# A two-layer encoder on one core: channel vectors behind the second weight block, bias tables negated once and fetched a slice early, a shared slot in each triangle

## The chip, the cores and the metric

The kernel runs on one core of one Trainium2 chip. The metric is the device time of one execution in microseconds, as the median of several runs. The kernel is one launch without loops on the device: the Python code is unrolled into 24029 instructions.

## The reference

Two post-norm layers over a sequence of 512 rows of 1024 channels, float32. In each layer one wide projection of the input feeds three mixers, whose results are projected, gated, summed, projected again, added to the input and normalised. A SwiGLU feed-forward part follows. Cut to its frame, with the part that the change touches:

```python
for l in range(DEPTH):
    h = einsum('bsd,de->bse', x, w_in[l])
    rq, rk, rv, rg, cq, ck, cv, dq, dk, dv, gates = split(h, splits)
    o_a = _retention(...)                    # 4 heads
    o_b = _chunk_attention(cq, ck, cv, ca_rel_bias[l])   # 8 heads
    o_c = _diff_attention(...)               # 4 heads, two softmaxes each
    g = sigmoid(gates + b_merge[l])
    merged = g[0] * (o_a @ w_a) + g[1] * (o_b @ w_b) + g[2] * (o_c @ w_c)
    x = _layer_norm(ALPHA * x + merged @ w_out[l], ln1_g[l], ln1_b[l])
    u_gate, u_up = split(x @ w_ffn_in[l])
    x = _layer_norm(ALPHA * x + (silu(u_gate) * u_up) @ w_ffn_out[l], ln2_g[l], ln2_b[l])

# in _chunk_attention, per head: a bias that depends on query minus key alone
idx = clip(qpos + pad - kpos, -REL_CLIP, REL_CLIP) + REL_CLIP
s = q @ k.T * d ** -0.5 + rel_bias[:, idx]
p = softmax(where(valid, s, -1e30))
```

## The kernel before

Every product runs in three matmuls (`mm3`, L108): each float32 operand is carried as a pair of float32r tiles, a high part that ScalarE casts (`part_hi`, L91) and a low part that VectorE subtracts (`part_lo`, L97). A weight block of up to 128x2048 (`Wt`, L113) is loaded by a DMA on the SyncE queue (SP) into a staging slot, one of 3, and split into `wh` (ScalarE, L138) and `wl` (VectorE, L139), 3 slots each.

The work is a list of items, written out by hand (L993 to L1009). Each item has one to three weight blocks and a function. `run_items` (L472) loads weight blocks so that three are ahead, calls the function, and lets it call `between()` in its middle and at its end, which emits the next group of side work (a head's softmax, a transposition and so on). So the program's order on each engine comes from this list. A scheduler at compile time then puts the instructions of each engine's queue in order by this program order and by when it reckons their inputs ready, so that one with ready inputs can go ahead of earlier ones; each queue runs in that order on the chip.

Activation tiles of 128x512 come from one pool of 61 slots (`g`, L75). A tile that finds no free slot waits, and so does what is queued behind its first instruction.

**The start** (`u_first`, L581). In layer 0, `run_items` first loads the first weight block in four pieces with the eight tiles of the transposed input between them (`load_x`, `split_x`), then the second and third block. Then `whole` (L591) loads two rotary tables (`ret_tables`, L564), emits `vectors()` (L523), and then projects by the first block: for each of the 8 input tiles k, six matmuls. The projections by the second and third block follow, 48 matmuls each. In layer 1 `halves` (L603) does it in halves of the columns, since the input comes out of the layer norm in halves.

`vectors()` loads seven rows of channel vectors with small DMAs (L531), clears their tile on GpSimd first (L526), turns them with one TensorE transpose (`pcol`, L535), copies the result out (L537), and derives a halved gate bias `hb` (L541), which the third block's gates need, and a scalar from four more DMAs (`lv`, L546).

**The chunk attention.** Its eight heads run as three slices each, `s_c1`, `s_c2`, `s_c3`, spread over nine items by `c(i)` (L977): in the middle of item i, `s_c3` of head i-2 and `s_c1` of head i; at its end `s_c2` of head i-1. The items are by turns a branch projection `u_branch(0, .)` and a query and key projection `u_cqk(.)`, then `u_vhl(dv)` and `u_dqk(0)`.

- `s_c1` (L785) loads the head's bias table `tb` as 128 overlapping rows of 512 out of one row of 768 (L789), negates it on ScalarE (L790), sets one corner (L791), and takes scores (`psc`, TensorE), the biased minimum (L350, VectorE), exp (L352, ScalarE) and the scaling by the sums (L799).
- `s_c2` (L803) transposes the triangle of scores (`ptr`, L365) and splits it into three pairs `cP`, six slots: blocks of 512, 512 and 256 columns.
- `s_c3` (L809) multiplies by the values (`pco`, L824), which waits for these splits.

**Gates.** The tanh tiles of some gates (`EARLY`, L45) are stored to memory and loaded again. `u_branch` (L955) calls `gate_of` (L941) for both of its halves first, so both loads (L945) come ahead of the first projection; L966 uses the tile after each.

Retention and differential attention have the same six-slot triangles (`s_r1`, L689; `s_d2`, L879).

Of the kernel before, what the change touches and what calls it, by code (L numbers as in the profile page):

```python
# [12 lines left out]
F32 = mybir.dt.float32  # L13
F32R = mybir.dt.float32r
# [3 lines left out]
P = 128  # L18
# [38 lines left out]
def trunk(ctx, tc, x_in, xT_in, w_in, ret_norm_g, da_norm_g, lq1, lk1, lq2, lk2, w_a, w_b, w_c, b_merge, w_out,  # L57
# [14 lines left out]
    nc.gpsimd.memset(mhalf, -0.5)  # L72
    saved = [dram.tile([S, D], F32, name=f"saved{i}") for i in range(2 * DEPTH - 1)]

    def g(dt=F32, name="g"):  # L75
        return gp.tile([P, 512], dt, tag="g", name=name)

# [6 lines left out]
    class Pair:  # L84


        def __init__(self, name="pr"):
            self.hi = g(F32R, name + "h")
            self.lo = g(F32R, name + "l")

    def part_hi(hi, src, scale=None):  # L91
        if scale is None:
# [420 lines left out]
    def layer(l):  # L513
# [6 lines left out]

        v = {}

        def vectors():  # L523

            rows = small.tile([64, P], F32, tag="rows", name="rows", bufs=1)
            nc.gpsimd.memset(rows, 0.0)  # L526
            r0 = 0
            for name, ap in (("bm", b_merge), ("rg", ret_norm_g), ("dg", da_norm_g), ("g1", ln1_g), ("b1", ln1_b),
                             ("g2", ln2_g), ("b2", ln2_b)):
                n = ap.shape[1] // P  # L530
                nc.sync.dma_start(rows[r0:r0 + n], ap[l:l + 1].rearrange("o (r c) -> (o r) c", c=P))  # L531
                v[name] = slice(r0, r0 + n)
                r0 += n
            psc = bank("pcol")
            nc.tensor.transpose(psc[:, :64], rows, ident[:64, :64])  # L535
            colv = small.tile([P, 64], F32, tag="colv", name="colv", bufs=2)
            nc.scalar.copy(colv, psc[:, :64])  # L537
            for name in list(v):
                v[name] = colv[:, v[name]]
            hb = small.tile([P, 24], F32, tag="hb", name="hb", bufs=2)  # L540
            nc.vector.tensor_scalar_mul(hb, v["bm"], 0.5)  # L541
            v["hb"] = hb

            lv = small.tile([P, 4, DA_DH], F32, tag="lv", name="lv", bufs=1)
            for j, vec in enumerate((lq1, lk1, lq2, lk2)):
                nc.sync.dma_start(lv[:, j], vec[l:l + 1].to_broadcast([P, DA_DH]))  # L546
            lp = small.tile([P, 2, DA_DH], F32, tag="lp", name="lp", bufs=1)
            for j in range(2):
                nc.vector.tensor_mul(lp[:, j], lv[:, 2 * j], lv[:, 2 * j + 1])
            ls = small.tile([P, 2], F32, tag="ls", name="ls", bufs=1)  # L550
            nc.vector.tensor_reduce(ls, lp, axis=mybir.AxisListType.X, op=ALU.add)
            le = small.tile([P, 2], F32, tag="le", name="le", bufs=1)
            nc.scalar.activation(le, ls, AF.Exp)
            nlam = small.tile([P, 1], F32, tag="nlam", name="nlam", bufs=2)
            nc.vector.tensor_sub(nlam, le[:, 1:2], le[:, 0:1])
            nc.vector.tensor_scalar_add(nlam, nlam, -lambda_init)
            v["nlam"] = nlam
# [23 lines left out]
        def u_first():  # L581

            def done(i, j, ps):
                if (i, j) == (0, 0):
                    xq.update({k: Quarters(xT[k], xT[k + 4]) for k in range(4)})
                if i < 2:
                    rqk_done((rq, rk)[i], j, ps)
                else:
                    gate_done(0, j, ps)

            def whole(*wts):  # L591
                ret_tables()
                vectors()
                banks = [bank("pt") for _ in range(2)]
                for k in range(KT):
                    for j in range(2):
                        a, c = xT[k], slice(P * j, P * j + P)
                        mm3(banks[j], wts[0].hi[:, k, c], wts[0].lo[:, k, c], a.hi, a.lo, k == 0, k == KT - 1)
                for i, w in enumerate(wts):
                    for j in range(2):  # L600
                        done(i, j, proj_T(xT, w, P * j) if i else banks[j])

            def halves(*wts):  # L603
                ret_tables()
                vectors()
                banks = [[bank("pt") for _ in range(2)] for _ in wts[:2]]
                proj_T_half0(xT, [(w, P * j, p[j]) for w, p in zip(wts, banks) for j in range(2)], {})
                banks.append([bank("pt") for _ in range(2)])
                proj_T_half0(xT, [(wts[2], P * j, banks[2][j]) for j in range(2)],
                             {2 * b: functools.partial(hooks[l], b) for b in range(4)})  # L610
                for i, (w, p) in enumerate(zip(wts, banks)):
                    for j in range(2):
                        done(i, j, proj_T(xT, w, P * j, ps=p[j], half=1))

            fn = whole if l == 0 else halves
            return [([wcols(c, 256)], KT) for c in (RQ, RK, GATE)], fn
# [68 lines left out]
        def s_r1(h):  # L685
            def fn():
                dh = g(name="dh")
                nc.sync.dma_start(dh, decay[h])
                rp[h] = [Pair("rp") for _ in range(3)]  # L689
                q, k = rq.pop(h), rk.pop(h)  # L690
                for b in range(3):
                    tmp = g(name="rtmp")
                    for mt in range(NT):
                        if PACK[mt][0] != b:
                            continue
                        o, w = PACK[mt][1], S - P * mt
                        ps = bank("psr")
                        msl = slice(P * mt, P * mt + P)
                        mm3(ps[:, :w], k.hi[:, msl], k.lo[:, msl], q.hi[:, P * mt:], q.lo[:, P * mt:], True, True)
                        nc.vector.tensor_mul(tmp[:, o:o + w], ps[:, :w], dh[:, :w])  # L700
                    w = PACKW[b]
                    split(rp[h][b], tmp[:, :w], cols=slice(0, w))
            return fn
# [67 lines left out]
            per = 256 // wd  # L771
            return dst[mt, h // per], (h % per) * 2 * wd

        cv, cqk, cE, cP = {}, {}, {}, {}
        ob = [None] * 4

        def u_cqk(p):
# [4 lines left out]
                cqk[p].set_k(proj_T(xT, wt, P))  # L782
            return [([wcols(CQ + P * p, P), wcols(CK + P * p, P)], KT)], fn

        def s_c1(h):  # L785
            def fn():
                tb = g(name="tb")
                src = rel[l, h:h + 1, 0:1]
                nc.sync.dma_start(tb, bass.AP(src.tensor, src.offset, [[1, P], [1, 512]]))  # L789
                nc.scalar.mul(tb, tb, -1.0)  # L790
                nc.vector.memset(tb[0:64, 0:64], -NEG)  # L791
                E = [g(name="cE") for _ in range(3)]
                sums = softmax_num(cqk[h // 2], h % 2, tb, E)
                r = small.tile([P, NT], F32, tag="rec", name="rec")
                nc.vector.reciprocal(r, sums)
                for nt in range(NT):
                    pk, c = PACK[NT - 1 - nt]
                    e = E[pk][:, c:c + P * (nt + 1)]
                    nc.vector.tensor_scalar_mul(e, e, r[:, nt:nt + 1])  # L799
                cE[h] = E  # L800
            return fn

        def s_c2(h):  # L803
            def fn():
                cP[h] = [Pair("cP") for _ in range(3)]
                transpose_triangle(cE.pop(h), cP[h])
            return fn

# [67 lines left out]

        def s_d2(h):
            def fn():
                dP[h] = [Pair("dP") for _ in range(3)]  # L879
                transpose_triangle(dE.pop(h), dP[h])  # L880
            return fn

# [72 lines left out]
        def u_branch(br, i):  # L955
            w = (w_a, w_b, w_c)[br][l]
            nk = w.shape[0] // P

            def fn(wt):
                act = (oa, ob, oc)[br]  # L960
                ts = [gate_of(br, 2 * i + j) for j in range(2)]
                for j in range(2):
                    d = 2 * i + j
                    ps = proj_T(act, wt, P * j, nk=nk)
                    t = ts[j]
                    nc.vector.scalar_tensor_tensor(t, t, 1.0, ps, op0=ALU.add, op1=ALU.mult)  # L966
                    if br == 0:
                        acc[d] = t
                    else:
                        nc.vector.tensor_add(acc[d], acc[d], t)  # L970
                    if br == 2:
                        mg[d] = Pair("mg")
                        split(mg[d], acc.pop(d), scale=0.5)
                    between()
            return [([w[:, 256 * i:256 * i + 256]], nk)], fn
# [306 lines left out]
```

## Time and profile before

| | |
|---|---|
| time, three runs | median 1947.54 us (1946.57 to 1952.31) |
| profiled execution | 1950.65 us, of which the span of instructions is 1948.8 us |
| mean granted TensorE clock | 0.998 |
| moved by DMA | 240.95 MB, 124 GB/s over the span |
| busy, of the span | TensorE 98%, weight loads 83%, VectorE 67%, ScalarE 45%, GpSimd 2% |

TensorE's row is the one to start from: it is nearly never idle, so a change can only pay where it removes one of its pauses or its work. For a pause, the profile names the instruction after it and what ended it. A matmul's busy time overlaps the next one's, so the pace of matmuls is read from the distance of their starts. A wait of another engine costs nothing by itself; it counts where TensorE's next instruction hangs on it.

### The profile page before, as it was taken

What the parts mean: (1) busy time and instruction counts of PE and PEld (TensorE: products, weight loads), DVE (VectorE), ACT (ScalarE), POOL (GpSimd) and SP (SyncE); (2) the same over time, 40 slices, a digit from 0 to 9 for tenths busy, and PEclk for the clock granted to TensorE, in tenths of its full rate; (3) what the DMA queues carried; (4) which work ended last, traced back from release to release, by engine and by line L of the source; (5) the groups of instructions that cost most, each with busy time, mean ns of one, the idle gap of its engine ahead of it and who ended that gap; (6) DMA issues with size and microseconds to landing.
All of it is one profiled execution on the core that took longest, in us unless ns stands there. A gap on an engine that the chain in (4) does not pass through costs nothing. (4 is left out here: it accounts for less than half of the span.)

```text
span 1948.8 us, 24029 instructions
## 1 busy us (share of the span) xinstructions
PE 1910.1 (98%) x9250; PEld 1608.0 (83%) x9250; DVE 1305.7 (67%) x2182; ACT 885.9 (45%) x1567; POOL 44.3 (2%) x73
## 2 busy tenths in 40 slices
PE   6999999999999999999999999999999999999998
PEld 5888887788888888888898888777888888888886
DVE  5776756667766756656578777566677557675666
ACT  4444445566743433333255454455676343333330
POOL 0000000000000000000000000000000000000000
PEclk9999999999999999999999999999999999999999
DMA  7353533222235434534434534331331634444341
GB/s 233 126 177 114 168 108 103 82 87 71 71 119 168 145 94 154 153 108 141 140 119 165 181 130 123 116 107 55 98 97 44 206 97 152 129 151 131 98 132 51
DMA packets 241782, 240.95 MB, mean 124 GB/s; under 512 B 8078, under 2 KB 180228, under 8 KB 241668
## 3 DMA queue, kind: packets, MB, share of 16 engines
q1 hardware_dynamic: 241668, 239.43, 38.8%
q8 instruction: 72, 1.18, 0.3%
q14 instruction: 42, 0.34, 0.1%
HBM read 224.72 MB, written 14.68 MB: 123 GB/s over the span
## 5 line engine op out<-in xcount | busy, mean ns | idle before, releaser
L109 PE MATMUL pt<-xTh,wh 128*128 128x512 f32 (+1 forms) x1584 | 597.0, 377 | 2.0 <-DVE mx L350 2.0
L110 PE MATMUL pt<-xTl,wh 128*128 128x512 f32 (+1 forms) x1584 | 593.5, 375 | 0.0
L111 PE MATMUL pt<-xTh,wl 128*128 128x512 f32 (+1 forms) x1584 | 593.4, 375 | 0.0
L138 ACT CAST wh<-st 128x1024 fp32r<-128x1024 f32 (+1 forms) x282 | 268.2, 982 | 276.6 <-issue 122.9
L139 DVE TENSOR_TENSOR wl<-st,wh 128x1024 fp32r<-128x1024 f32 (+1 forms) x282 | 313.5, 1135 | 103.5 <-ACT wh L138 103.4
L109 PEld LDWEIGHTS pt<-xTh,wh 128*128 128x128 f32 x1584 | 298.6, 189 | 54.4 <-DVE mx L350 2.5
L111 PEld LDWEIGHTS pt<-xTh,wl 128*128 128x128 f32 x1584 | 298.6, 189 | 53.9
L110 PEld LDWEIGHTS pt<-xTl,wh 128*128 128x128 f32 x1584 | 298.9, 189 | 51.9
L212 ACT CAST wh<-st 128x1024 fp32r<-128x1024 f32 x64 | 65.2, 1051 | 98.9 <-PE pt L110 64.9
L1076 DVE TENSOR_TENSOR fth<-fth,pt 128x512 f32<-128x512 f32 x44 | 30.2, 685 | 104.5 <-PE pt L111 104.5
L213 DVE TENSOR_TENSOR wl<-st,wh 128x1024 fp32r<-128x1024 f32 x64 | 76.6, 1220 | 8.8 <-ACT wh L212 8.6
L212 ACT CAST wh<-sa 128x1024 fp32r<-128x1024 f32 x48 | 49.5, 1050 | 66.8 <-PE pt L110 62.5
L1074 ACT ACTIVATE fth<-pt 128x512 f32<-128x512 f32 x44 | 26.3, 597 | 107.6 <-PE pt L111 107.6
L300 ACT COPY sw<-pt 32x512 f32<-32x512 f32 (+1 forms) x96 | 55.6, 579 | 41.5 <-PE pt L111 40.3
L213 DVE TENSOR_TENSOR wl<-sa,wh 128x1024 fp32r<-128x1024 f32 x48 | 57.8, 1219 | 21.0 <-ACT wh L212 21.0
L1075 DVE SCALAR_TENSOR_TENSOR fth<-fth,pt 128x512 f32<-128x512 f32 x44 | 30.1, 683 | 57.7 <-ACT fth L1074 57.7
L109 PE MATMUL pt<-oah,wh 128*128 128x512 f32 x128 | 51.2, 400 | 0.0
L109 PE MATMUL pn<-wh,xTh 128*128 128x512 f32 x128 | 50.4, 394 | 0.0
L110 PE MATMUL pt<-oal,wh 128*128 128x512 f32 x128 | 50.1, 392 | 0.2
L109 PE MATMUL pf<-wh,s12h 128*128 128x512 f32 x128 | 50.0, 391 | 0.0
L111 PE MATMUL pt<-oah,wl 128*128 128x512 f32 x128 | 49.9, 390 | 0.0
L111 PE MATMUL pn<-wh,xTl 128*128 128x512 f32 x128 | 49.9, 390 | 0.0
(262 smaller groups left out, 3473.9 us busy)
## 6 DMA issues: line engine op xcount, KB each, us to landing
st<-in_w_in SPq DMA_DIRECT2D x63, 1024.0 KB
st<-in_w_ffn_in SPq DMA_DIRECT2D x88, 512.0 KB
st<-in_w_ffn_out SPq DMA_DIRECT2D x28, 1024.0 KB
st<-in_w_in SPq DMA_DIRECT2D x32, 512.0 KB
th<-th SPq DMA_DIRECT2D x48, 256.0 KB
st<-in_w_branch_a SPq DMA_DIRECT2D x8, 1024.0 KB
st<-in_w_out SPq DMA_DIRECT2D x8, 1024.0 KB
saved<-z SPq DMA_DIRECT2D x24, 256.0 KB
```

The lines of the kernel that those rows point to most:

```text
L109: nc.tensor.matmul(ps, lh, rh, start=start, stop=False)
L110: nc.tensor.matmul(ps, lh, rl, start=False, stop=False)
L111: nc.tensor.matmul(ps, ll, rh, start=False, stop=stop)
L138: done = [nc.scalar.copy(self.hi[:, a:b], st[:, a:b]), nc.vector.tensor_sub(self.lo[:, a:b], st[:, a:b], f(self.hi[:, a:b]))]
L139: nc.vector.tensor_sub(self.lo[:, a:b], st[:, a:b], f(self.hi[:, a:b]))]
L212: nc.scalar.copy(self.hi[:, s], st[:, s])
L213: nc.vector.tensor_sub(self.lo[:, s], st[:, s], f(self.hi[:, s]))
L300: nc.scalar.copy(sw[half * b:half * b + half], ps[half * o:half * o + half])
L1074: nc.scalar.activation(t, pg, AF.Tanh, scale=0.5)
L1075: nc.vector.scalar_tensor_tensor(t, t, 1.0, pg, op0=ALU.add, op1=ALU.mult)
L1076: nc.vector.tensor_mul(t, t, pu)
```

## The change

Four edits.

1. `vectors()` is emitted after the projection by the second weight block in layer 0, and after the first halves in layer 1.
2. At the head of layer 0's `vectors()`, all bias rows are loaded (128 rows of 96), negated by one VectorE instruction and stored to a scratch tensor `nrel`. `s_c1` no longer negates; it takes a table that `bias_table` has loaded from `nrel` in the slice of the head before (head 0's own table is loaded in its own slice).
3. The third pair of every triangle takes the two halves of one slot (`HalfPair`), so five slots instead of six.
4. `u_branch` loads a gate just ahead of the half that uses it.

```diff
+    nrel = dram.tile([P, 96], F32, name="nrel")
...
+    class HalfPair:
+        def __init__(self, name="pr"):
+            t = g(F32R, name)
+            self.hi, self.lo = t[:, :256], t[:, 256:]
+
+    def triangle(name):
+        return [Pair(name), Pair(name), HalfPair(name)]
...
+        def negate_bias():
+            t = small.tile([P, 96], F32, tag="nrel", name="nrel", bufs=1)
+            nc.sync.dma_start(t, rel.rearrange("l h (r c) -> (l h r) c", c=96))
+            nc.vector.tensor_scalar_mul(t, t, -1.0)
+            nc.sync.dma_start(nrel, t)
+
         def vectors():
+            if l == 0:
+                negate_bias()
...
             def whole(*wts):
                 ret_tables()
-                vectors()
...
                     for j in range(2):
                         done(i, j, proj_T(xT, w, P * j) if i else banks[j])
+                    if i == 1:
+                        vectors()
...
             def halves(*wts):
                 ret_tables()
-                vectors()
...
                              {2 * b: functools.partial(hooks[l], b) for b in range(4)})
+                vectors()
...
-                rp[h] = [Pair("rp") for _ in range(3)]
+                rp[h] = triangle("rp")
...
+        def bias_table(h):
+            ctb[h] = g(name="tb")
+            r = 768 // 96 * (CA_HEADS * l + h)
+            src = nrel[r:r + 1, 0:1]
+            nc.sync.dma_start(ctb[h], bass.AP(src.tensor, src.offset, [[1, P], [1, 512]]))
+
         def s_c1(h):
             def fn():
-                tb = g(name="tb")
-                src = rel[l, h:h + 1, 0:1]
-                nc.sync.dma_start(tb, bass.AP(src.tensor, src.offset, [[1, P], [1, 512]]))
-                nc.scalar.mul(tb, tb, -1.0)
+                if h == 0:
+                    bias_table(0)
+                if h + 1 < CA_HEADS:
+                    bias_table(h + 1)
+                tb = ctb.pop(h)
                 nc.vector.memset(tb[0:64, 0:64], -NEG)
...
-                cP[h] = [Pair("cP") for _ in range(3)]
+                cP[h] = triangle("cP")
...
-                dP[h] = [Pair("dP") for _ in range(3)]
+                dP[h] = triangle("dP")
...
-                ts = [gate_of(br, 2 * i + j) for j in range(2)]
                 for j in range(2):
                     d = 2 * i + j
+                    t = gate_of(br, d)
                     ps = proj_T(act, wt, P * j, nk=nk)
-                    t = ts[j]
```

More of the change, by code (lines that the diff above doesn't have):

```diff
@@ L772, in v_of @@
             return dst[mt, h // per], (h % per) * 2 * wd
-        cv, cqk, cE, cP = {}, {}, {}, {}
+        cv, cqk, cE, cP, ctb = {}, {}, {}, {}, {}
         ob = [None] * 4
```

## The prediction

> **What bounds the kernel now.** I read the page's first part, then TensorE's waits, then a table of windows by stage, then the timeline wherever that table shows TensorE idle.
>
> ```profile
> span 1948.8 us, 24029 instructions
> PE 1910.1 (98%) x9250; PEld 1608.0 (83%) x9250; DVE 1305.7 (67%) x2182; ACT 885.9 (45%) x1567; POOL 44.3 (2%) x73
> ```
>
> ```profile
> PE pcol L535 <- DMA rows<-in_ln_b: 16.6, 1, 16.6
> PE pco L824 <- ACT cPh L93: 9.2, 6, 2.0
> PE pt L109 <- DVE mx L350: 2.0, 2, 1.1
> ```
>
> ```profile
> 6.00:21.70 15.70, 0.00 (x0) 0.01 (x1) 9.92 (x13) 9.95 (x14) 0.00 (x0) 1.00 0.89 300
> 21.70:27.30 5.60, 5.58 (x14) 4.32 (x15) 2.06 (x6) 0.21 (x1) 0.20 (x1) 1.00 0.36 114
> 266.00:390.00 124.00, 118.02 (x581) 97.83 (x579) 75.67 (x175) 65.78 (x136) 2.08 (x4) 0.99 0.31 98
> 1228.00:1372.00 144.00, 138.41 (x686) 114.38 (x685) 87.95 (x202) 77.78 (x162) 3.12 (x6) 1.00 0.31 99
> ```
>
> The wait rows give total, times, longest. The window rows give the length, then busy time and count of PE, PEld, DVE, ACT and POOL, then the granted clock, the DMA share and GB/s. TensorE is the bound, idle for 1948.8 - 1910.1 = 38.7 us in all. Three rows hold 27.8 us of that: one wait of 16.6 us for a channel vector, and eight short ones in the chunk attention of both layers. By windows, those two stages idle 124.00 - 118.02 = 5.98 and 144.00 - 138.41 = 5.59 us, together 11.6. The change aims at exactly these places and takes no matmul away, so its ceiling is about 28 us plus what the clock gives back.
>
> **The start.** The timeline of all engines (start, length, engine, line, in square brackets the idle time before it and its releaser) and one row of the SP queue's waits:
>
> ```profile
> 1.48 3.68 PE L494 MATMUL warm<-ident 128*128 128x128 f32 x16 [1.48 <-POOL ident masks.py:199]
> 5.21 0.69 DVE L507 TENSOR_TENSOR xTl<-xf,xTh 128x512 fp32r<-128x512 f32 x1
> 8.91 1.17 SPq L132 DMA_DIRECT2D st<-in_w_in  x2
> 13.73 0.69 DVE L507 TENSOR_TENSOR xTl<-xf,xTh 128x512 fp32r<-128x512 f32 x1
> 16.80 1.04 ACT L138 CAST wh<-st 128x1024 fp32r<-128x1024 f32 x1 [3.10 <-DMA st<-in_w_in]
> 17.75 0.61 ACT L506 CAST xTh<-xf 128x512 fp32r<-128x512 f32 x1
> 19.02 0.69 DVE L507 TENSOR_TENSOR xTl<-xf,xTh 128x512 fp32r<-128x512 f32 x1
> 19.62 3.52 DVE L139 TENSOR_TENSOR wl<-st,wh 128x1024 fp32r<-128x1024 f32 x3
> 21.72 0.34 PE L535 MATMUL pcol<-ident,rows 64*128 64x64 f32 x1 [16.57 <-DMA rows<-in_ln_b]
> 22.22 0.38 SPq L132 DMA_DIRECT2D st<-in_w_in  x1
> 27.28 0.40 PE L109 MATMUL pt<-xTh,wh 128*128 128x512 f32 x1
> 27.51 0.40 PE L110 MATMUL pt<-xTl,wh 128*128 128x512 f32 x1
> 35.01 1.18 ACT L300 COPY sw<-pt 64x512 f32<-64x512 f32 x2 [7.26 <-PE pt L111]
> 36.20 2.00 ACT L138 CAST wh<-st 128x1024 fp32r<-128x1024 f32 x2
> ```
>
> ```profile
> SPq L531 <- DMA st<-in_w_in: 6.8, 4, 2.7
> ```
>
> The first input tile is split at 5.21 + 0.69 = 5.9 us, the seventh at 13.73 + 0.69 = 14.4, the eighth at 19.02 + 0.69 = 19.7 (its cast stands in ScalarE's queue behind the second block's, which waits for its DMA). All that time TensorE stands at the transpose: its rows' small loads are queued on SP behind the weights and wait for weights to land. The first block's result reaches ScalarE at 35.01.
>
> Without the transpose in front, TensorE follows the input. I reckon at two paces: 14 matmuls in 5.58 us, 0.40 each, right after the long pause, and 27.51 - 27.28 = 0.23 afterwards. Tile 7 comes last, at 19.7; its six matmuls take 6 x 0.23 = 1.4 us and the result is out at 21.3, where it was 35.0: **13.7 us** saved. The slow opening of 14 x (0.40 - 0.23) = 2.4 us, which the 35.0 contains, now lies under the wait for input tiles. Blocks two and three are split by 19.62 + 3.52 = 23.1 and are used from 21.1 and 32.0 (48 x 0.23 = 11.0 a block), so they follow without a gap, if the second's half that is cut last (first of the three subtractions, about 20.8) is counted.
>
> Bounds: if the whole first block ran at 0.40, it would end at 5.9 + 48 x 0.40 = 25.1, result 25.3, saving 9.7. If the eighth tile were split ahead of the second block, TensorE itself would limit: 5.9 + 14 x 0.40 + 34 x 0.23 = 19.3, saving 15.5. I keep 13.7, since these rows' order of splits is not edited.
>
> [...]
>
> What moves with `vectors()`: eleven loads, the memset, the transpose, its copy, `hb` and the scalar. The transpose keeps its 0.34 us of TensorE, now between blocks two and three. `hb` is needed after the third block's first half, 24 x 0.23 = 5.5 us after the transpose, against a copy and one small VectorE operation: covered. In layer 1 the transpose stands in no wait row and moves by a few matmuls: nothing.
>
> `negate_bias` adds two DMAs and one VectorE instruction, unseen in the trace. The instruction is 96 columns, a sixth of the 0.69 us rows above in size: 0.1 to 0.7 us, 0.2 taken, off TensorE's path. The store on SP waits for load and negation; behind it on SP are the seven rows, `lv` and the fourth weight block, which now goes out at 22.22. TensorE needs that block at 21.3 + 2 x 11.0 = 32 plus 11 = 43 rather than at 57. The second block took 16.80 - 8.91 = 7.9 us to land in the crowded start; with 6 us of delay for the load and store the fourth lands at 36 and is cast and subtracted by 41. (Its cast at 36.20 was not limited by landing but by the first block's slot, which comes free 13.7 us earlier.) Zero is taken; if that cover were gone, each microsecond past 43 costs one, I allow 0 to 3.
>
> **The chunk attention.** Here are what touches the bias table, two slices of layer 0 in the timeline, and SP's waits for slots:
>
> ```profile
> L790 ACT ACTIVATE tb<-tb x16: 631/632/633, 278.4 to 1347.7; 128x512 f32<-128x512 f32 x16
>   DMA tb<-in_rel: 57.3, 16
>   ACT tb L790: 38.0, 16
> ```
>
> ```profile
> 322.87 0.63 ACT L790 ACTIVATE tb<-tb 128x512 f32<-128x512 f32 x1 [2.52 <-DMA tb<-in_rel]
> 324.63 0.72 ACT L352 ACTIVATE cE<-cE,mx 128x512 f32<-128x512 f32 x1 [1.13 <-DVE mx L350]
> 328.15 2.00 ACT L138 CAST wh<-st 128x1024 fp32r<-128x1024 f32 x2
> 331.37 1.35 ACT L93 CAST cPh<-ptr 128x512 fp32r<-128x512 f32 x3
> 332.01 0.50 PE L824 MATMUL pco<-cPh,vhl 128*128 128x512 f32 x1 [1.27 <-ACT cPh L93]
> 332.34 0.40 PE L335 MATMUL psc<-ks,qs 128*128 128x512 f32 x1
> 334.26 0.37 SPq L789 DMA_DIRECT2D tb<-in_rel  x1
> 339.67 0.69 DVE L966 SCALAR_TENSOR_TENSOR th<-th,pt 128x512 f32<-128x512 f32 x1 [3.56 <-DMA th<-th]
> 340.08 1.25 PE L365 MATMUL ptr<-ident,cE 128*128 128x128 f32 x10
> 340.79 0.63 ACT L790 ACTIVATE tb<-tb 128x512 f32<-128x512 f32 x1 [5.40 <-DMA tb<-in_rel]
> 342.39 0.50 PE L109 MATMUL pt<-xTh,wh 128*128 128x512 f32 x1 [1.06 <-DVE mx L350]
> ```
>
> ```profile
> SPq L945 <- DVE cPl L99: 11.6, 4, 5.4
> SPq L789 <- PE psc L336: 4.7, 6, 1.5
> ```
>
> The chain: SP issues the table late (334.26), it lands 6.5 us later, ScalarE stands still in front of it (5.40), then VectorE (38.0 us over 16 heads). ScalarE then works without a break from 324.63 to the cast of `cPh` at 331.37, which the matmul at 332.01 awaits. With the table there a slice early, ScalarE loses 57.3 us of waits and 16 x 0.632 = 10.1 us of work, except head 0 of each layer, which still waits. Per slice it comes 2.5 to 5.4 + 0.6 us earlier to its queue, against pauses of at most 2.0 us: all six `pco` waits go, 9.2 us. For the two of `pt`, VectorE's `th` wait is next: it ends at 340.36, then the corner and the first minimum, 0.8 us, 341.2; TensorE's transposes end about 341.1. So 0.1 of each stays: 1.8 us gone. Each pause also slowed the next matmul by 332.34 - 332.01 - 0.23 = 0.1: 0.8 for eight. Sum 11.8; I take **10.5**, since ScalarE can only start on a head when its scores exist, and a tenth is kept for that. Bounds: 0, if another wait steps in at each place, and 11.6 + 0.8 = 12.4.
>
> Four edits alter slots. In the middle of an item, the triangle holds one less, the next head's table one more, and the second gate tile is fetched after the table instead of before: level. The second gate's load is one 256 KB table later; it is used 24 matmuls (5.5 us) after the first, so it is covered unless SP stalls. The triangles of the other two mixers lie where TensorE hardly waits: zero.
>
> **Sum.** 13.7 + 10.5 = 24.2 us. On the profiled execution 1950.65 becomes 1926.4; that one is 3.1 above the median, and from the median 1947.54 it gives **1923.3 us**.
>
> **Rivals.** (a) Clock: the first block runs slowly throughout: 9.7 + 10.5, 1927.3. For it: the first 14 matmuls did so after 3.68 us of warming transposes. Against: work is then nearly continuous. 0.12. (b) The chunk attention's idle time stays, the gate loads taking the table's place: only 13.7, 1933.8. For it: VectorE already stands 3.56 us before a gate. Against: it is ScalarE's lateness that TensorE awaits. 0.17. (c) The change doesn't do what it says: the transpose is put ahead again, since queues are ordered by reckoned readiness. Then its rows, behind load, negation and store, come up to 6.5 + 0.2 later, and 10.5 - 6.7 = 3.8 is left, 1943.7. Against: higher-priority matmuls fill TensorE once the input is there. 0.07. (d) Slower: the early table finds no slot and holds SP with the second gate and the next weight block behind it. Price: 14 early fetches, each beyond its cover of 5.5 us; it turns the sum at 5.5 + 24.2 / 14 = 7.2 us a fetch. At one and a half times the longest slot wait seen (8.1) it would cost 14 x 2.6 = 36.4, 1959.7. Against: 5.4 is the longest, and slots are level. 0.04.
>
> **How the numbers follow.** The forecast has 0.60. A measurement here can tell about 0.3%, 5.8 us, from no change. Faster: forecast, (a) and (b), 0.89; within: (c), 0.07; slower: (d), 0.04. The range goes from 1947.5 - 15.5 - 12.4 = 1919.6, less 1.6 for scatter, to (b)'s 1933.8 plus 2.7: 1918.0 to 1936.5.
>
> **What would show it.** Right: the first projection starts near 6 us, the first rotary copy near 21; `pcol` leaves the wait list and comes after about 96 matmuls; no ACT instruction at the table, `tb` waits under 10 us; `pco` waits near none; both windows above idle under 1 us. Wrong: a wait at the first block over 5 us, `th` or SP slot waits of several microseconds each, or a fourth block that TensorE awaits.

## The result and the profile after

The changed kernel takes 1923.55 us, median of four runs (1922.15 to 1924.10); the kernel before 1948.37, median of four (1946.57 to 1952.31; the three of the table above and one more). The ratio is 0.9869, 95% interval 0.9852 to 0.9886, which is 25.5 us (22.2 to 28.8). The profiled execution took 1923.79 us.

The head of the page after, then TensorE's waits (line numbers of the changed kernel: L122 to L124 are the three matmuls, L151 and L152 the split of a weight block, L519 and L520 that of an input tile, L854 the value product):

```profile
span 1922.0 us, 23998 instructions
PE 1907.8 (99%) x9250; PEld 1606.2 (84%) x9250; DVE 1305.7 (68%) x2183; ACT 876.8 (46%) x1551; POOL 46.2 (2%) x73
```

```profile
PE pt L122 <- ACT xTh L519: 1.5, 2, 1.2
PE pt L123 <- DVE xTl L520: 1.1, 2, 0.8
PE pco L854 <- DVE cPl L112: 0.7, 2, 0.3
```

The same 9250 matmuls; idle time fell from 38.7 to 1922.0 - 1907.8 = 14.2 us. The 16.6 us in front of `pcol` are gone, and of the chunk attention's 11.2 us two waits of together 0.7 are left. Its two windows, moved with the work (columns as in the prediction):

```profile
250.00:375.00 125.00, 124.54 (x619) 103.65 (x618) 80.78 (x190) 65.91 (x141) 2.90 (x6) 1.00 0.33 97
1214.00:1357.00 143.00, 142.66 (x706) 119.32 (x705) 91.28 (x208) 75.62 (x158) 4.17 (x8) 1.00 0.31 99
```

They idle 0.46 and 0.34 us where it was 5.98 and 5.59. What is left of the table's waits, from the groups that touch it, and the two largest rows of SP's waits in front of table loads (L812) and gate loads (L975):

```profile
L821 DVE MEMSET tb<- x16: 112/112/112, 264.9 to 1304.8; 64x64 f32 x16
  DMA tb<-nrel: 5.5, 4
```

```profile
SPq L812 <- PE pco L854: 10.3, 6, 3.3
SPq L975 <- DVE cPl L112: 8.6, 6, 3.3
```

The start, in the timeline after, all engines:

```profile
5.41 0.49 PE L122 MATMUL pt<-xTh,wh 128*128 128x512 f32 x1 [0.25 <-ACT xTh L519]
6.71 0.39 PE L122 MATMUL pt<-xTh,wh 128*128 128x512 f32 x1
6.94 0.40 PE L123 MATMUL pt<-xTl,wh 128*128 128x512 f32 x1
15.63 0.39 PE L124 MATMUL pt<-xTh,wl 128*128 128x512 f32 x1
15.65 1.05 ACT L151 CAST wh<-st 128x1024 fp32r<-128x1024 f32 x1 [3.09 <-DMA st<-in_w_in]
16.60 0.61 ACT L519 CAST xTh<-xf 128x512 fp32r<-128x512 f32 x1
17.27 0.50 PE L122 MATMUL pt<-xTh,wh 128*128 128x512 f32 x1 [1.25 <-ACT xTh L519]
18.61 0.50 PE L123 MATMUL pt<-xTl,wh 128*128 128x512 f32 x1 [0.84 <-DVE xTl L520]
18.70 1.99 ACT L151 CAST wh<-st 128x1024 fp32r<-128x1024 f32 x2 [0.54 <-DMA st<-in_w_in]
19.75 0.63 PE L123 MATMUL pt<-xTl,wh 128*128 128x512 f32 x1
20.18 0.63 PE L124 MATMUL pt<-xTh,wl 128*128 128x512 f32 x1
20.72 1.17 ACT L313 COPY sw<-pt 64x512 f32<-64x512 f32 x2
32.49 0.27 PE L556 MATMUL pcol<-ident,rows 64*128 64x64 f32 x1
32.88 2.01 ACT L151 CAST wh<-st 128x1024 fp32r<-128x1024 f32 x2
```

TensorE begins at 5.41, at full pace from the third matmul on (6.94 - 6.71 = 0.23). At 16.0 it has done seven input tiles and waits for the eighth, whose cast (16.60) stands behind the second block's (15.65, held up 3.09 us by its DMA). After two pauses of 1.25 and 0.84 us it runs at half pace (20.18 - 19.75 = 0.43). The first rotary copy comes at 20.72, before at 35.01. It no longer shows when TensorE's result is there: before, ScalarE waited for TensorE, now the copy follows a cast that ends at 18.70 + 1.99 = 20.69. The transposition waits for nothing, and the fourth block's cast (32.88) is early enough.

Matched matmul by matmul, TensorE is 13.5 us ahead of the kernel before from the third block on, 21.2 after layer 0's chunk attention, and 27.0 after layer 1's: 13.5 from the start, 7.7 and 6.0 from the two stages (with 0.2 lost in between).

### The profile page after: what moved, and what is told of

The parts are those of the page before. It is cut to its first block, busy times and chain, and to the rows that moved or that the text cites. A ratio compares the mean times of both kernels' runs of the same rounds, so it can differ in the third digit from the quotient of the medians.

```text
span 1922.0 us, 23998 instructions
## 1 busy us (share of the span) xinstructions
PE 1907.8 (99%) x9250; PEld 1606.2 (84%) x9250; DVE 1305.7 (68%) x2183; ACT 876.8 (46%) x1551; POOL 46.2 (2%) x73
## 5 line engine op out<-in xcount | busy, mean ns | idle before, releaser
L122 PE MATMUL pt<-xTh,wh 128*128 128x512 f32 (+1 forms) x1584 | 596.8, 377 | 1.5 <-ACT xTh L519 1.5
L124 PE MATMUL pt<-xTh,wl 128*128 128x512 f32 (+1 forms) x1584 | 593.2, 375 | 0.0
L151 ACT CAST wh<-st 128x1024 fp32r<-128x1024 f32 (+1 forms) x282 | 268.6, 981 | 272.3 <-issue 138.8
L152 DVE TENSOR_TENSOR wl<-st,wh 128x1024 fp32r<-128x1024 f32 (+1 forms) x282 | 314.0, 1137 | 106.8 <-ACT wh L151 106.3
L122 PEld LDWEIGHTS pt<-xTh,wh 128*128 128x128 f32 x1584 | 298.3, 189 | 54.4 <-ACT xTh L519 2.3
L124 PEld LDWEIGHTS pt<-xTh,wl 128*128 128x128 f32 x1584 | 298.4, 188 | 53.6
L313 ACT COPY sw<-pt 32x512 f32<-32x512 f32 (+1 forms) x96 | 55.6, 580 | 33.5 <-PE pt L124 26.5
L365 ACT ACTIVATE cE<-cE,mx 128x512 f32<-128x512 f32 (+1 forms) x64 | 35.3, 553 | 38.7 <-DVE mx L363 38.4
L122 PE MATMUL pt<-oah,wh 128*128 128x512 f32 x128 | 51.2, 400 | 0.0
L122 PE MATMUL pn<-wh,xTh 128*128 128x512 f32 x128 | 50.4, 394 | 0.0
L124 PE MATMUL pt<-oah,wl 128*128 128x512 f32 x128 | 50.0, 391 | 0.0
L122 PE MATMUL pf<-wh,s12h 128*128 128x512 f32 x128 | 50.0, 390 | 0.0
```

The source lines that it names most:

```text
L122: nc.tensor.matmul(ps, lh, rh, start=start, stop=False)
L124: nc.tensor.matmul(ps, ll, rh, start=False, stop=stop)
L151: done = [nc.scalar.copy(self.hi[:, a:b], st[:, a:b]), nc.vector.tensor_sub(self.lo[:, a:b], st[:, a:b], f(self.hi[:, a:b]))]
L152: nc.vector.tensor_sub(self.lo[:, a:b], st[:, a:b], f(self.hi[:, a:b]))]
L313: nc.scalar.copy(sw[half * b:half * b + half], ps[half * o:half * o + half])
L365: nc.scalar.activation(e, e, AF.Exp, bias=m, scale=-1.0, accum_out=sums[:, nt:nt + 1])
```

## The experiments

The theory: two separate gains, the start's and the chunk attention's, the latter from the table's landing. Its rivals: one gain feeds the other; the freed slot or the late gate load is what makes the early table possible; ScalarE's negations were the cost. Each ratio is to the kernel before on the same chip; the changed kernel's own is 0.9869, and two ratios are compared, as the runs came from several chips.

**The first edit alone.**

```diff
             def whole(*wts):
                 ret_tables()
-                vectors()
...
+                    if i == 1:
+                        vectors()
```

> The kernel before with the first edit alone (vectors behind the second weight block). Theory, two separate gains: the start gives 13.5 us, as the trace after shows from the third weight block on, so 13.5 us below the kernel before, first rotary copy near 21 us; the chunk attention keeps its eight pauses of TensorE, about 11 us of waits. Rival, the start pays for the chunk attention too (everything downstream shifts and its waits shrink): 20 us or more below before. Rival, the start's gain is given back later: under 8 us below.

Measured: 1937.22 us, ratio 0.9930 (0.9918 to 0.9943): 13.6 us. TensorE's waits:

```profile
PE pco L825 <- ACT cPh L93: 9.3, 6, 2.0
PE pt L109 <- DVE mx L350: 2.0, 2, 1.0
```

The start's gain came in full, and the eight pauses stayed to the tenth. The two do not touch each other.

**The bias edit alone**, with `vectors()`, triangles and gates as before, and `negate_bias()` behind the second block.

```diff
+                    if i == 1:
+                        negate_bias()
...
+                if h == 0:
+                    bias_table(0)
+                if h + 1 < CA_HEADS:
+                    bias_table(h + 1)
+                tb = ctb.pop(h)
```

> The kernel before with the bias edit alone: tables negated once behind the second block, fetched from there a slice early, no negation on ScalarE; channel vectors in their old place, full triangles, both gates loaded first. Theory, two separate gains: TensorE still waits 16.6 us at the transposition of the channel vectors, the chunk attention is nearly free of pauses, 13.3 us below the kernel before. Rival, the early table needs the slot that the shared triangle frees: SP waits for slots and the gain is under 8 us.

Measured: 1935.73 us, ratio 0.9928 (0.9914 to 0.9942): 14.0 us. TensorE's waits:

```profile
PE pcol L543 <- DMA rows<-in_ln_b: 15.4, 1, 15.4
PE pco L842 <- ACT cPh L95: 0.6, 2, 0.3
```

The stage's gain is whole without shared slots and without late gates. 0.9930 x 0.9928 = 0.9859, inside the interval of the whole change: the two add up.

**The table in its own slice.**

```diff
-                if h == 0:
-                    bias_table(0)
-                if h + 1 < CA_HEADS:
-                    bias_table(h + 1)
+                bias_table(h)
```

> The changed kernel, but each head's table is fetched in its own slice, from the negated copy. Theory, the table's landing is what ScalarE and VectorE waited for, and the negation only 0.63 us behind it: VectorE waits for the table 2 to 5 us a head, each pause of TensorE shrinks by the 0.63 us and the 0.1 us of the hand-over, about half of the chunk attention's gain is lost, 5 to 8 us slower than the changed kernel (1929 to 1932 where it has 1923.5). Rival, ScalarE's negations alone made it late: as fast as the changed kernel within 1.5 us. Rival, the early fetch is all: 12 us or more slower.

Measured: 1933.38 us, ratio 0.9917 (0.9903 to 0.9930), 9.4 us more than the change's. The traces, matched matmul by matmul, tell more than these two ratios with their intervals: the two stages lose 5.6 and 5.5 us, 11.1 together, of which 1.4 is hidden in the time: this run's start is that much faster, with shorter pauses before the last input tile (0.7 us the longest) and no half pace after them. So my theory's 5 to 8 is too small, the first rival is wrong, and the second, with its 12 or more, is nearly right. TensorE's waits, the table's wait, and a stretch of TensorE's timeline:

```profile
PE pco L851 <- ACT cPh L106: 5.5, 4, 2.3
PE pco L851 <- DVE cPl L112: 1.5, 4, 0.6
```

```profile
  DMA tb<-nrel: 22.3, 14
```

```profile
347.80 0.50 PE L851 MATMUL pco<-cPh,vhl 128*128 128x512 f32 x1 [2.21 <-ACT cPh L106]
349.06 0.63 PE L851 MATMUL pco<-cPl,vhl 128*64 128x512 f32 x1
349.48 0.42 PE L348 MATMUL psc<-ks,qs 128*128 128x256 f32 x1
```

The pauses left come to 7.0 us, somewhat over the 5.4 that stay of 11.2 if each of eight shrinks by 0.73. What I had left out stands in the last rows: after the pause of 2.21 us a matmul of 512 columns takes 349.48 - 349.06 = 0.42 us instead of 0.23, and that lasts until about 352. Layer 1 has a pause of 2.30 us, and its granted clock over 1214 to 1357 us is 0.99, in the changed kernel 1.00. So these two pauses cost more than their length: the 7.0 us of pauses, 0.1 each for the matmuls after eight of them and twice 1.6 us of half pace (a price that the account below reads from two traces) make 11.0 of the 11.1. Of the 13.7 us that the two stages gave, that leaves 2.6 for sparing the negation alone; the early fetch brings the rest.

**Negation by ScalarE at each use**, the fetch a slice early from the bias itself.

```diff
-            if l == 0:
-                negate_bias()
...
-            src = nrel[r:r + 1, 0:1]
+            src = rel[l, h:h + 1, 0:1]
...
                 tb = ctb.pop(h)
+                nc.scalar.mul(tb, tb, -1.0)
```

> The changed kernel, but tables are fetched a slice early from the bias itself and ScalarE negates each at its use; no negation up front. Theory, the landing is what counted: ScalarE has 16 x 0.63 = 10 us of work more, off TensorE's path, 0 to 2 us slower than the changed kernel. Rival, ScalarE's work was it: 6 us or more slower. The start should be as in the changed kernel, since the load and store of the negated tables are hidden there; if they cost something, this one is faster by it.

Measured: 1922.62 us, ratio 0.9860 (0.9846 to 0.9873). No slower than the change. With the table there early, sixteen negations of 0.63 us, and the load and store up front, are off TensorE's path alike; the early fetch does it all.

**Six slots again; both gates first again.**

```diff
-        return [Pair(name), Pair(name), HalfPair(name)]
+        return [Pair(name) for _ in range(3)]
```

```diff
+                ts = [gate_of(br, 2 * i + j) for j in range(2)]
                 for j in range(2):
                     d = 2 * i + j
-                    t = gate_of(br, d)
+                    t = ts[j]
```

> The changed kernel with six slots in every triangle again. Theory: slots are level and the sharing pays nothing by itself; within 2 us of the changed kernel, SP's waits for a slot in front of gate and table loads a few microseconds more in total. Rival: the early table lives on the freed slot; SP's waits in front of tables and second gates grow to several microseconds each, TensorE waits for the splits of the triangle again, 5 us or more slower than the changed kernel.

> The changed kernel with both gates loaded at the head of the branch projection again. Theory: the second gate is covered either way; within 1.5 us of the changed kernel. Rival: the later load is what lets the next table come early (the second gate's 256 KB stand in front of it otherwise and hold a slot): tables are waited for again, 3 us or more slower.

Measured: 1924.05 us, ratio 0.9869 (0.9855 to 0.9884), and 1923.46 us, ratio 0.9866 (0.9852 to 0.9881). Neither edit moves the time. With six slots SP's waits in front of tables and gates come to 34.4 us instead of 33.5, and VectorE's for the table to 6.8 instead of 5.5, but TensorE's do not grow:

```profile
SPq L975 <- PE pco L854: 11.6, 6, 3.7
SPq L812 <- PE pco L854: 11.4, 8, 3.3
```

**Channel vectors behind the first block.**

```diff
-                    if i == 1:
+                    if i == 0:
                         vectors()
```

> The changed kernel with the channel vectors behind the first weight block instead of the second. Theory: the rows' loads, behind load, negation and store on SP (the last issued at 21.55 us in the changed kernel), land 2 to 7 us after their issue, while TensorE is done with the first block at 20.9: it waits 3 to 7 us at the transposition and runs some microseconds at half pace after it, 4 to 9 us slower than the changed kernel. Rival: small loads land fast enough once the queue runs, or the transposition finds another place: within 1.5 us.

Measured: 1928.23 us, ratio 0.9891 (0.9876 to 0.9906), 4.3 us more than the change's. TensorE's timeline:

```profile
23.52 0.37 PE L556 MATMUL pcol<-ident,rows 64*128 64x64 f32 x1 [1.85 <-DMA rows<-in_ln_b]
24.41 0.63 PE L123 MATMUL pt<-xTl,wh 128*128 128x512 f32 x1
24.84 0.63 PE L124 MATMUL pt<-xTh,wl 128*128 128x512 f32 x1
```

The rows were awaited for 1.85 us only, less than the 3 to 7 expected. But the half pace that had set in before the last input tile (0.43 a matmul) goes on to 29.1 us (granted clock 0.90 over 21.7 to 60 us), where in the changed kernel it ends at 22.4. The place behind the second block is right: the rows need it.

**Input tiles first.** In the start, the second and third block's splits keep their place behind the last input tile.

```diff
-                if beside is not None:
+                if beside is not None or keep:
                     for ins in done:
                         tc.keep_in_program_order(ins)
...
-                ready[-1].append(sp() if callable(sp) else Wt(*sp, beside=(load_x, split_x) if first else None))
+                ready[-1].append(sp() if callable(sp) else Wt(*sp, beside=(load_x, split_x) if first else None, keep=at == 1))
```

> The changed kernel, but in the start the casts and subtractions of the second and third weight block keep their place behind the last input tile, where the scheduler had put the second block's first cast ahead of it. Theory: TensorE's two pauses before the last input tile (1.25 and 0.84 us), and nine matmuls at half pace after them (9 x 0.20 us), come from that cast's wait for its DMA; without them the last tile is split near 14 us, TensorE does block one without a pause, then waits for block two, split near 18 us, 1 to 2 us once; 0 to 3 us faster than the changed kernel. Rival: the DMA limits the start, the pauses move to block two in full and nothing is won: within 0.5 us.

Measured: 1920.57 us (1920.13 to 1921.07), ratio 0.9853 (0.9837 to 0.9870). All its runs lie below all four of the change (1922.15 to 1924.10), though on another chip; by the ratios it is 3.1 us faster, but their intervals overlap. By traces TensorE is 3.45 us ahead of the changed kernel in the second block. Its timeline there:

```profile
18.29 0.50 PE L124 MATMUL pt<-xTh,wl 128*128 128x512 f32 x1 [0.51 <-DVE wl L152]
18.62 0.40 PE L122 MATMUL pt<-xTh,wh 128*128 128x512 f32 x1
18.86 0.40 PE L123 MATMUL pt<-xTl,wh 128*128 128x512 f32 x1
```

One wait of half a microsecond in place of two longer ones, and full pace after it. At the end of the trace 3.4 us of the lead are left.

**Both together**: input tiles first, and negation at each use instead of up front (the two edits above).

> The kernel with the input tiles split ahead of the second block (as in the run with that edit alone, 1920.6 us), and without the negation up front: tables are fetched early from the bias itself and negated one by one on ScalarE. Theory: landing and order are what counted, the negation costs nothing either way; 1920 to 1921.5 us. Rival: both gains share a cause in the crowded start, and this one is 1 us or more faster than 1920.6, or ScalarE's 10 us of work return as 1 us or more.

Measured: 1920.64 us, ratio 0.9852 (0.9835 to 0.9868), the same as with input tiles first alone. It does without the scratch tensor.

**Pauses on purpose**, a single execution of the changed kernel with waits put in; most of its extra time is the waits themselves. In calls 3, 5, 7, 9, 11, 13 and 15 of the feed-forward projection of each layer, the next matmul is made to wait:

```diff
+        pauses = {3: 0, 5: 1, 7: 2, 9: 3, 11: 4, 13: 5, 15: 7}
...
+                for _ in range(pauses[count[0]]):
+                    nc.scalar.copy(t, src)
+                    src = t
+                w = wt.hi[:, 0, 0:1]
+                nc.vector.scalar_tensor_tensor(w, src[:, 0:1], 0.0, f(w), op0=ALU.mult, op1=ALU.add)
```

> The changed kernel with seven pauses of rising length put between feed-forward projections of each layer: a chain of 0 to 7 ScalarE copies of the block before, then an exact rewriting of one weight column, which the next projection's first matmul reads; the result is the same. It measures what a pause of TensorE costs beyond itself, by the distance of matmul starts after it. Theory from the pauses seen so far (2.05 and 2.21 us followed by matmuls 0.43 apart, 1.27 and 1.49 us not): pauses over some 2 us are followed by 1.5 to 3.5 us at half pace, shorter ones by none; where a pause of about 2 us falls on either side is chance. [...]

Measured: 2047.87 us. The copies stood behind other work on ScalarE and VectorE, so the pauses came out at 0.94 twice and at 5.3 to 10.2 twelve times: nothing between, so this run alone cannot test the theory's 2 us. TensorE's timeline after one of each:

```profile
653.82 0.47 PE L122 MATMUL pt<-xTh,wh 128*128 128x512 f32 x1 [0.94 <-ACT wh L151]
654.13 0.39 PE L123 MATMUL pt<-xTl,wh 128*128 128x512 f32 x1
654.36 0.40 PE L124 MATMUL pt<-xTh,wl 128*128 128x512 f32 x1
...
808.12 0.80 PE L122 MATMUL pt<-xTh,wh 128*128 128x512 f32 x1 [5.27 <-DVE wh L1143]
808.71 0.63 PE L123 MATMUL pt<-xTl,wh 128*128 128x512 f32 x1
809.14 0.63 PE L124 MATMUL pt<-xTh,wl 128*128 128x512 f32 x1
...
812.54 0.39 PE L123 MATMUL pt<-xTl,wh 128*128 128x512 f32 x1
812.77 0.40 PE L124 MATMUL pt<-xTh,wl 128*128 128x512 f32 x1
```

The pause of 5.27 us was followed by nine matmuls at half pace (0.43 a matmul; up to 812.5 us, 4.4 us and longer than the theory's 3.5), 2.1 us lost beyond the pause (812.77 - 808.12 less 11 x 0.23); the one of 0.94 by none (0.23). Over the whole span the granted clock is 0.974, in the changed kernel 0.998. Pauses of about 2 us, from the other kernels, stand in the last section.

## Why the prediction was right

The forecast was 1923.3 us, the measured median is 1923.55. Its two places were the right ones, and each was shown alone: 13.6 and 14.0 us in the kernels that make one edit each. The sum of 24.2 lies within the interval of the saving (22.2 to 28.8), but below what the two traces differ by in span (26.8). That the medians agree to 0.3 us is luck: for the profiled execution the sum gave 1926.4, and the changed kernel's took 1923.79; the 3.1 us by which the profiled execution of before lay above its median made up for it. Point by point:

**The start**, 13.7 forecast, 13.5 by the trace, and this nearness is in part luck too. TensorE's last matmul of the first block starts at 20.18 us instead of 35.26, which is 15.1 earlier. Two errors of mine had made the saving too small: the eighth tile is split at 18.6, not 19.7, and I set 35.0, the end of the first of the block's two column halves, against 21.3, the end of the second, which in the kernel before comes 0.7 later. What I left out takes it back: nine matmuls after the pauses at the last tile ran at half pace (9 x 0.20 = 1.8 us), well into the second block, which leaves 14.0, and the transposition, which I had counted as moved at no cost, takes 0.4 between blocks two and three. The slow opening that I took over from the kernel before did not occur. Where it did (the kernel with the table in its own slice, 0.43 a matmul up to 10.6 us), it lay under the wait for input tiles, as forecast. That the last tile's place in ScalarE's queue set the end was right; the run that restores that place is 3.4 us faster by the traces.

**`negate_bias`** taken at zero: right, as the ratios with and without it show (0.9869 and 0.9860, 0.9853 and 0.9852). SP's 5.5 us of waiting at the store held up nothing that was due.

**The chunk attention**, 10.5 forecast, 13.7 in the two stages by the trace: the mis-sized term. The waits of 9.2 and 2.0 went as the step said. I then added 0.1 us to each pause for the matmul after it and took a tenth off, which was not needed; what I missed is half pace after the longest pause. The kernel before has it, in TensorE's timeline:

```profile
364.75 0.50 PE L824 MATMUL pco<-cPh,vhl 128*128 128x512 f32 x1 [2.05 <-ACT cPh L93]
...
366.48 0.63 PE L824 MATMUL pco<-cPl,vhl 128*64 128x512 f32 x1
366.90 0.42 PE L335 MATMUL psc<-ks,qs 128*128 128x256 f32 x1
```

0.42 for 512 columns again, after a pause of 2.05, with a granted clock of 0.50 from 365.19 to 368.60 us. Two traces give its price: the kernel with the first edit alone has the same pause in layer 0 (2.03 us) without half pace after it (512 columns in 0.23 us), and from this pause to the next transposes its lead over the kernel before grows by 1.6 us. The idle time of the two windows fell by 10.8 us (from 11.6 to 0.8); with 0.8 for the matmuls after the pauses and this 1.6 that makes 13.2 of the 13.7, and 0.5 stays unexplained. The row was there to be read before the forecast; I had looked at the pace after the pause at 332, which was full (0.23 for 512 columns).

**Slots, gates, triangles** at zero: right, and shown by undoing each. The early table needs no freed slot.

**Rivals.** (a) named the right force at the wrong place: the half pace (0.43 a matmul) came after the two pauses of 1.25 and 0.84 us at the last tile, not from the first matmul on, and cost under 2 us, not 4. (b) did not occur: both gates loaded first cost nothing either. (c) did not occur; the transposition came after 96 matmuls. (d) did not: SP's waits in front of tables and gates grew from 20 to 33.5 us in sum, but none is over 3.4, under the 5.5 of cover.

## What to carry to other kernels

Where one engine is 98% busy, list its pauses with what ended them; each is a separate sum, and edits that touch none of them (here shared slots, later gate loads, and fewer negations once the table comes early) can be left at zero. A pause of TensorE can cost more than its length: half pace after one of 2.05 us cost 1.6 us more here and after one of 5.27 us 2.1, and the two of 1.25 and 0.84 us at the start were followed by 1.8 us of it, while none came after the pauses of 2.04 and 2.03 us. Look at the distance of starts and the granted clock behind each one. For a load that something waits on, its place in the queue mattered more here than what is done to the data: fetching a slice early gave everything that negating up front seemed to give, while negating up front without the early fetch gave 2.6 of 13.7 us.

## What the runs showed of the hardware

Behind some pauses of TensorE the matmuls of 512 columns ran at half pace, 0.42 to 0.43 us apart instead of 0.23. The length of the pause alone does not tell which:

| pause, us | where | distance of starts after it, about |
|---|---|---|
| 0.98 to 1.49, six of them | the kernel before, both layers' chunk attention | 0.23 (granted clock 1.00) |
| 2.05 | the kernel before, layer 0 | 0.42 (granted clock 0.50 from 365.19 to 368.60) |
| 2.04 | the kernel before, layer 1 | 0.23 (granted clock 1.00) |
| 2.03 | the first edit alone, layer 0 | 0.23 |
| 2.21 | the table in its own slice, layer 0 | 0.42, to about 352 |
| 1.25 and 0.84, a matmul apart | the changed kernel, start | 0.43 (granted clock 0.50 from 18.99 to 22.41) |
| 0.51 | input tiles first, start | 0.23 |
| 0.94 | pauses on purpose | 0.23 |
| 5.27 | pauses on purpose | 0.43, to 812.5 |

Here are windows of the kernel before around its pauses of 2.05 and 2.04 us, each as long as the stretch at half clock, 3.41 us (length, then busy time of PE, PEld, DVE, ACT and POOL, granted clock, DMA share, GB/s):

```profile
361.78:365.19 3.41, 1.36 (x7) 0.82 (x6) 2.14 (x5) 2.24 (x5) 0.00 (x0) 1.00 0.25 90
365.19:368.60 3.41, 3.41 (x14) 2.94 (x13) 1.27 (x3) 0.27 (x1) 0.00 (x0) 0.50 0.31 101
1324.34:1327.75 3.41, 1.91 (x11) 1.69 (x12) 2.32 (x4) 2.18 (x5) 0.00 (x0) 1.00 0.04 10
1327.75:1331.16 3.41, 3.41 (x19) 2.91 (x18) 1.29 (x2) 0.58 (x1) 0.00 (x0) 1.00 0.65 215
```

In the first row TensorE is idle for 3.41 - 1.36 = 2.05 us, the whole first pause, and the next row has half the clock. In the third row it is idle for 1.50 us, as the second pause began before it, and the clock stays at 1.00. At the start of the changed kernel, 15.58 to 18.99 us has both pauses, 2.09 us idle, and half the clock behind it; at the end of the kernel before, with its last matmuls, 1938.74 to 1942.15 us has 1.88 us idle, and the clock stays at 1.00 up to 1945.56. Why the clock fell after the pause of 2.05 us and not after that of 2.04, no run shows. (Ahead of its first recorded change a trace gives the clock as 1.00, so the window 21.70:27.30 of the kernel before reads 1.00 although its matmuls ran at half pace, 0.43 a matmul.)

The opening differs from run to run. Right behind the 16 transposes the matmuls of 512 columns ran 0.23 us apart almost from the first in six kernels with an early start (the changed kernel, the first edit alone, negation at each use, six slots, input tiles first, vectors behind the first block), and 0.43 apart for some nine matmuls in two, the pauses on purpose and the kernel with the table in its own slice:

```profile
7.15 0.63 PE L122 MATMUL pt<-xTh,wh 128*128 128x512 f32 x1
7.58 0.63 PE L123 MATMUL pt<-xTl,wh 128*128 128x512 f32 x1
```

In the changed kernel the first entry of the clock record, 1.00, starts at 5.34 us, ahead of the first of these matmuls at 5.41. On the time the opening has little effect, since the eighth input tile, the last to be split, ends the block either way.
